# A hybrid decoder block on one core: two more warm-up products, the first weights on the scalar queue, fh and fl at another place in the partition, two orders on TensorE

## The chip, the cores and the metric

The kernel runs on one core of one Trainium2 chip. The metric is the device time of one execution in microseconds; for the kernel before, three runs gave 446.09 to 446.27, median 446.21.

## The reference, cut to what matters

256 tokens, width 1024, float32, one layer:

```
n = rmsnorm(x, norm1_g)
cu, cg, q, k, v, gc, ga = split(n @ w_in)
y_conv = silu(layernorm(causal_conv31(cu * sigmoid(cg)))) @ w_conv_out
y_attn = attention(rmsnorm(q), rmsnorm(k), v, ALiBi, causal, 8 heads of 128) @ w_attn_out
h = x + (sigmoid(gc) * y_conv + sigmoid(ga) * y_attn) @ w_out
out = h + (silu(n2 @ w_gate) * (n2 @ w_up)) @ w_down      # n2 = rmsnorm(h, norm2_g), inner width 2816
```

With 256 tokens in blocks of 256, only a token's own block is attended.

## The kernel before, in words

Every matrix product is made of two token tiles of 128 by chunks of 512 output columns, over k-tiles of 128. For accuracy each operand is split into a high part (rounded to the float32r type) and a low rest, and three products are summed: high by high, low by high, high by low. `mm3` (L133) issues them: the activations (`xh`, `xl`, for example xgh and xgl, or fh and fl) are the stationary operand, the weights (`hi` = whi, `lo` = wlo) move, 512 columns each.

The weights come in pieces of two k-tiles; one piece is one slot of the run loop at the end (L663). In a slot TensorE does six products for token tile 0, then the `jobs` of the slot, then six for token tile 1, then the `post` jobs. `pre` and `late` jobs stand ahead of the slot and behind it. So the place of a job in one of these lists decides where in TensorE's stream its small products break the row of big ones. `stream_dma` (L100) issues the loads of a piece (raw), `stream_split` (L113) makes whi on ScalarE (L123) and wlo on VectorE or POOL (L124), six slots ahead.

The start (L601 to L643) is written out by hand. x comes transposed as xt, in five parts that SP issues between the first weights; the gain of norm1 is an extra column in each of its rows of 257 numbers. `split_x` makes xgh on ScalarE and xgl on VectorE. `square` squares x on ScalarE (sq and xsq, L627 and L630), where xsq of parts 2 and 3 stands behind whi of piece 3, and POOL adds the squares up (L631, L633). `first_norm` is a post job of slot 4: four tiny products ss (L648) sum over the partitions with a column `ones`, which POOL sets at L643. The norm's factor rstd is applied later to the results. Ahead of all this eight warm-up products of zeros (wps, L161) run on TensorE while nothing has landed.

Further places that the change touches: `norm_back` (L299) turns the normalised conv output back with four transposes (yb) for two k-tiles and makes yh and yl of it; four such groups are spread over jobs and post of two slots (L247). `score` (L383) makes the scores sc of a head by two products, a narrow one for query tile 0 and a wide one of 256 columns for query tile 1. In the feed-forward, gu are the gate and up products with hh and hl as stationary operands, dn the down products with fh and fl; the last pieces of dn for token tile 1 are computed in two halves of 256 columns named end.

Where a tile lies in a partition follows from the sizes of the pools, which are laid out one behind the other: constants, weights (raw, whi, wlo), the pairs (xg, y, ao, m, h), small tiles, then the pool of the early stages, whose place is taken by fh and fl later. In the built kernel whi, wlo and the pairs begin at a multiple of 512 bytes, fh and fl 32 bytes behind one.

Of the kernel before, what the change touches and what calls it, by code (L numbers as in the profile page):

```python
# [9 lines left out]
F32 = mybir.dt.float32  # L10
F32R = mybir.dt.float32r
BF16 = mybir.dt.bfloat16
AF = mybir.ActivationFunctionType
# [3 lines left out]
P = 128  # L17
D = 1024
S = 256
T = S // P  # L20
H = 8
KC = 31
FF = 2816
KD = D // P
KF = FF // P
CW = 512
G = 2
EPS = 1e-6
# [13 lines left out]
AHEAD = 6  # L42
# slots after which the next heads follow
HEAD_STEP = ((0, 3, 6, 9), (0, 3, 5, 7))
# weights of the work, by which the taps are dealt out over the slots
SLOT = 2.6
# [4 lines left out]
REFILL = 2  # L51
WARM = 8
TABLE_SLOT = 57


class Chunk:
    """CW output columns of one product, for all tokens: nk k-tiles in pieces of G."""

# [6 lines left out]
def hybrid_block(ctx: ExitStack, tc: tile.TileContext, x, xT, par, w_in, w_co, w_ao, w_o, w_gu, w_dn, out):  # L65
    nc = tc.nc

    cst = ctx.enter_context(tc.tile_pool(name="cst", bufs=1))
    wp = ctx.enter_context(tc.tile_pool(name="wp", bufs=1))
    t8 = ctx.enter_context(tc.tile_pool(name="t8", bufs=2))  # L70
    sm = ctx.enter_context(tc.tile_pool(name="sm", bufs=2))
# [5 lines left out]
    def bank(name, *shape):  # L77
        return ps.tile([P, *shape], F32, tag="tr", bufs=2, name=name)

# [1 line left out]
    slots = []  # L81
# [4 lines left out]
    def add(*chunks):  # L86
        """One chunk, or two of which each half is done in turn."""
        n = chunks[0].nk // G
        parts = [range(n)] if len(chunks) == 1 else [range(n // 2), range(n // 2, n)]
        for part in parts:  # L90
            for c in chunks:
                slots.extend((c, g) for g in part)
# [7 lines left out]
    def stream_dma(upto):  # L100
        while at["dma"] < min(upto, len(slots)):
            i = at["dma"]
            c, g = slots[i]
            raw[i] = wp.tile([P, G, CW], F32, tag="raw", bufs=RAW_BUFS, name=f"raw{i}")
            for part in parts(i):
                nc.sync.dma_start(raw[i][:, part, :], c.w[g][:, part, :])
                between(i, part)
            at["dma"] += 1
# [24 lines left out]
    def mm3(c, i, g, t, acc=None, cols=slice(0, CW), first=0, last=None):  # L133
        """Piece g of the chunk for token tile t; the sum runs from k-tile first to last."""
        xh, xl = c.lhs()
        acc = c.acc[t] if acc is None else acc
        last = c.nk - 1 if last is None else last
        tok = slice(t * P, (t + 1) * P)
        for j in range(G):
            k = g * G + j  # L140
            nc.tensor.matmul(acc, xh[:, k, tok], hi[i][:, j, cols], start=(k == first), stop=False)  # L141
            nc.tensor.matmul(acc, xl[:, k, tok], hi[i][:, j, cols], start=False, stop=False)  # L142
            nc.tensor.matmul(acc, xh[:, k, tok], lo[i][:, j, cols], start=False, stop=(k == last))  # L143

# [1 line left out]
    prm = cst.tile([P, N_PAR], F32, name="prm")  # L146
    xt = ea.tile([P, KD, S + 1], F32, tag="vs", name="xt")
    xs = cst.tile([P, T, D], F32, name="xs")

# [1 line left out]
    warm = cst.tile([P, CW], BF16, name="warm")  # L151
    nc.vector.memset(warm, 0.0)
    tiny = cst.tile([P, 1], F32, name="tiny")

    def load_table(func):
        nc.scalar.activation(tiny, warm[:, :1], func)

    load_table(AF.Sigmoid)
    wps = bank("wps", CW)
    for _ in range(WARM):  # L160
        nc.tensor.matmul(wps, warm[:, :P], warm, start=True, stop=True)  # L161
    ident = cst.tile([P, P], F32, name="ident")
    make_identity(nc, ident)
    mhalf = cst.tile([P, 8], F32, name="mhalf")
    nc.gpsimd.memset(mhalf, -0.5)
# [10 lines left out]
    def rsqrt_mean(o, ss, n, width):  # L176
        """o = (ss / n + EPS) ** -0.5"""
        nc.gpsimd.tensor_scalar(o, ss, 1.0 / n, EPS, op0=ALU.mult, op1=ALU.add)
        nc.gpsimd.tensor_tensor(o, o, mhalf[:, :width], op=ALU.pow)

# [1 line left out]
    xg, aoT, yT, mT, hT = {}, {}, {}, {}, {}  # L182
# [7 lines left out]

# [1 line left out]
    cacc, ca = {}, {}  # L192
# [12 lines left out]
    def refill(ch):  # L205
        """The channels of the next tile go on the partitions, after KC - 1 zeros."""
        j, cv = ch["next"], ch["cv"]
        for t in range(T):
            nc.tensor.transpose(cv[:, KC - 1 + t * P : KC - 1 + (t + 1) * P],
                                ca[j // 2][:, t, (j % 2) * P : (j % 2 + 1) * P], ident)  # L210
        cacc[j] = ea.tile([P, S], F32, tag="cacc", bufs=4, name=f"cacc{j}")
        ch["j"], ch["k"], ch["next"] = j, 0, j + 2
# [11 lines left out]
    def run_taps(slot, until):  # L224
        while load["dve"] + TAP <= until:
            live = [ch for ch in chains if ch["j"] is not None]
            if not live:
                return
            load["turn"] += 1
            ch = live[load["turn"] % len(live)]  # L230
            conv_tap(ch)
            load["dve"] += TAP if len(live) > 1 else TAP_ALONE
            if ch["k"] == KC:
                j, ch["j"] = ch["j"], None
                want_refill(slot, ch)
                if j % 2:
                    last = j == KD - 1
                    at_ = slot + 3
                    while not last and busy[at_] > 1:
                        at_ += 1  # L240
                    busy[at_] += 1
                    jobs[at_].append(lambda p=j // 2: norm_stats(p))
                    pe_side[at_] += 0.45
                    dve_side[at_] += 0.7
                    if last:
                        for i in range(4):
                            (post if i % 2 else jobs)[at_ + 2 + i // 2].append(lambda i=i: norm_back(2 * i))  # L247

# [66 lines left out]

# [1 line left out]
    vs = {}  # L317
# [49 lines left out]
    def head(first, slot, h):  # L367
# [3 lines left out]
        s = {}  # L371
# [11 lines left out]
        def score():  # L383
            s["bias"] = sm.tile([P, 3, P], F32, tag="bias", name=f"bias{h}")
            nc.scalar.mul(s["bias"], dist, 2.0 ** (-8.0 * (h + 1) / H))
            s["sc"] = bank(f"sc{h}", 4, P)
            nc.tensor.matmul(s["sc"][:, 0, :], s["q"][:, :P], s["k"][:, :P], start=True, stop=True)
            nc.tensor.matmul(s["sc"][:, 1:3, :], s["q"][:, P:], s["k"], start=True, stop=True)
            most()
# [50 lines left out]

# [1 line left out]
    sgs = ea.tile([P, 2, T, D], F32, tag="sgs", name="sgs")  # L442
# [21 lines left out]

# [1 line left out]
    def merge_done(b):  # L466
# [26 lines left out]

# [1 line left out]
    s2 = sm.tile([P, T, 2], F32, bufs=1, name="s2")  # L495

# [37 lines left out]

# [1 line left out]
    ff = {}  # L536
# [42 lines left out]

# [1 line left out]
    for p in range(KD // 2):  # L581
# [18 lines left out]

# [1 line left out]
    xg[0] = pair("xg")  # L602

    def load_x(k0, k1):
        nc.sync.dma_start(xt[:, k0:k1, :], xT[:, k0:k1, :])

    def between(i, part):
        if i == 0:
            load_x(part.start, part.stop)
            if part.stop == G:  # L610
                load_x(2, 4)
        elif i < KD // 2 - 1 and part.stop == G:
            load_x(2 * i + 2, 2 * i + 4)

    def split_x(k):
        g = xt[:, k, S:]
        nc.scalar.activation(xg[0][0][:, k, :], xt[:, k, :S], AF.Copy, scale=g)
        nc.vector.scalar_tensor_tensor(xg[0][1][:, k, :], xt[:, k, :S], g, xg[0][0][:, k, :].bitcast(F32),
                                       op0=ALU.mult, op1=ALU.subtract)

    stream_dma(AHEAD)
    sq = ea.tile([P, 2, S], F32, tag="yt", name="sq0")

    def square(q):
        """Squares of x, summed over the parts of its rows that share a partition."""
        if q == 0:
            nc.scalar.activation(sq, xt[:, :2, :S], AF.Square)  # L627
            return
        s = sm.tile([P, 2, S], F32, tag="u", name=f"xsq{q}")
        nc.scalar.activation(s, xt[:, 2 * q : 2 * q + 2, :S], AF.Square)  # L630
        nc.gpsimd.tensor_add(sq, sq, s)  # L631
        if q == KD // 2 - 1:
            nc.gpsimd.tensor_add(sq[:, 0, :], sq[:, 0, :], sq[:, 1, :])  # L633

    for i in range(6):
# [4 lines left out]
        if i >= 2:  # L640
            square(i - 2)
    ones = cst.tile([P, 1], F32, name="ones")
    nc.gpsimd.memset(ones, 1.0)  # L643

    def first_norm():
# [12 lines left out]

# [1 line left out]
    n = len(slots)  # L660
# [85 lines left out]
```

## Time and profile before

| what | |
|---|---|
| time, median of 3 runs | 446.21 us |
| profiled execution, its span from the first to the last instruction | 443.5 us |
| TensorE (PE) busy | 437.6 us, 99% |
| weight loads of TensorE (PEld) busy | 359.6 us |
| VectorE (DVE) busy | 309.6 us |
| ScalarE (ACT) busy | 243.9 us |
| GpSimd (POOL) busy | 87.5 us |
| moved by DMA | 80.21 MB, 181 GB/s on average |

The page gives the span of one profiled execution; the time of a run has in addition what lies around the span, 2.7 us here against the median. Busy times are no proof of a bound by themselves: products are pipelined and overlap in the records, so the distance from one start to the next tells more than a duration. L12 is line 12 of the kernel.

### The profile page before, as it was taken

The page shows a single profiled execution, that of the slowest core. Times are in us where ns is not written, and L with a number is a line of the kernel's source. Part 1 is how long each engine was busy: PE and PEld are TensorE (multiplying, and loading weights), DVE is VectorE, ACT ScalarE, POOL GpSimd, SP SyncE. Part 2 cuts the span into 40 slices and gives each one's busy share as a digit, 9 for nine tenths or more (in the row PEclk, how much of TensorE's full clock was granted, in tenths as well). Part 3 has the DMA queues.
Part 4 walks back from the last instruction along what each step waited for, and adds up shares of the span by engine and source line. Part 5 has one row for each costly group of instructions (what it writes and reads, how often), then busy time and mean ns, then how long its engine had stood idle before and what let it go on. Part 6 is the DMA issues. An engine that isn't in the chain of part 4 may idle for free.

```text
span 443.5 us, 5743 instructions
## 1 busy us (share of the span) xinstructions
PE 437.6 (99%) x2026; PEld 359.6 (81%) x2026; DVE 309.6 (70%) x523; ACT 243.9 (55%) x439; POOL 87.5 (20%) x73
## 2 busy tenths in 40 slices
PE   8999999999999999999999999999999999999997
PEld 4788888888888888888888888888888888888886
DVE  5989999898899799967586575555555555644501
ACT  6854466689998676639325374444444444633200
POOL 1614465745462443100000000000000000000000
PEclk9999999999999999999999999999999999999999
DMA  8986684355345444544837337655555555585001
GB/s 274 345 271 213 211 303 150 144 185 197 142 149 185 142 137 150 190 163 161 293 95 247 133 120 253 196 189 184 184 185 179 187 181 184 184 252 204 25 0 49
DMA packets 23340, 80.21 MB, mean 181 GB/s; under 512 B 2576, under 2 KB 3216, under 8 KB 23312
## 3 DMA queue, kind: packets, MB, share of 16 engines
q1 hardware_dynamic: 22896, 78.66, 52.9%
q10 hardware_dynamic: 416, 1.19, 0.8%
q8 instruction: 16, 0.26, 0.3%
q14 instruction: 12, 0.10, 0.1%
HBM read 78.79 MB, written 1.05 MB: 180 GB/s over the span
## 4 chain that ended last, share of the span: by engine, by line
PE 94%; POOL 2%; ACT 2%; DMA 1%; SPq 0%; issue 0%; DVE 0%
PE gu L141 9%; PE gu L143 9%; PE gu L142 9%; PE dn L141 4%; PE dn L143 4%; PE dn L142 4%; PE g L143 3%; PE g L142 3%; PE g L141 3%; PE conv L141 2%; PE conv L143 2%; PE conv L142 2%; PE k L143 2%; PE v L143 2%; PE q L143 2%; PE q L141 2%
## 5 line engine op out<-in xcount | busy, mean ns | idle before, releaser
L124 DVE TENSOR_TENSOR wlo<-raw,whi 128x1024 fp32r<-128x1024 f32 (+1 forms) x125 | 153.0, 1256 | 30.5 <-ACT whi L123 29.6
L123 ACT CAST whi<-raw 128x1024 fp32r<-128x1024 f32 (+1 forms) x149 | 148.9, 1035 | 34.9 <-PE dn L142 19.8
L221 DVE SCALAR_TENSOR_TENSOR cacc<-cv,prm,cacc 128x256 f32<-128x256 f32 x240 | 97.2, 475 | 0.2
L141 PE MATMUL gu<-whi,hh 128*128 128x512 f32 x176 | 69.6, 395 | 0.0
L124 POOL TENSOR_TENSOR wlo<-raw,whi 128x1024 fp32r<-128x1024 f32 x24 | 58.1, 2426 | 54.5 <-ACT whi L123 49.6
L143 PE MATMUL gu<-wlo,hh 128*128 128x512 f32 x176 | 68.7, 390 | 0.0
L142 PE MATMUL gu<-whi,hl 128*128 128x512 f32 x176 | 68.5, 389 | 0.0
L143 PEld LDWEIGHTS gu<-wlo,hh 128*128 128x128 f32 x176 | 33.0, 188 | 7.1
L142 PEld LDWEIGHTS gu<-whi,hl 128*128 128x128 f32 x176 | 33.1, 188 | 6.6
L141 PEld LDWEIGHTS gu<-whi,hh 128*128 128x128 f32 x176 | 33.1, 188 | 6.4
L141 PE MATMUL dn<-whi,fh 128*128 128x512 f32 x82 | 32.5, 396 | 0.0
L143 PE MATMUL dn<-wlo,fh 128*128 128x512 f32 x82 | 32.4, 396 | 0.0
L142 PE MATMUL dn<-whi,fl 128*128 128x512 f32 x82 | 32.4, 396 | 0.0
L546 ACT ACTIVATE fs<-gu,rstd 128x256 f32<-128x256 f32 x22 | 10.4, 475 | 39.1 <-PE gu L143 39.1
L548 DVE SCALAR_TENSOR_TENSOR f<-gu,rstd,fs 128x256 f32<-128x256 f32 x22 | 10.6, 484 | 29.1 <-ACT fs L546 29.1
L141 PE MATMUL conv<-whi,xgh 128*128 128x512 f32 x64 | 26.1, 409 | 0.9 <-ACT whi L123 0.8
L141 PE MATMUL g<-whi,xgh 128*128 128x512 f32 x64 | 26.6, 415 | 0.0
L142 PE MATMUL conv<-whi,xgl 128*128 128x512 f32 x64 | 25.4, 398 | 0.0
L143 PE MATMUL conv<-wlo,xgh 128*128 128x512 f32 x64 | 25.4, 397 | 0.0
L143 PE MATMUL g<-wlo,xgh 128*128 128x512 f32 x64 | 25.2, 394 | 0.0
L142 PE MATMUL g<-whi,xgl 128*128 128x512 f32 x64 | 25.0, 391 | 0.0
L561 ACT CAST fh<-ftr 128x512 fp32r<-128x512 f32 x11 | 6.5, 587 | 23.9 <-PE ftr L560 23.9
(159 smaller groups left out, 746.4 us busy)
## 6 DMA issues: line engine op xcount, KB each, us to landing
raw<-in_w_in SPq DMA_DIRECT2D x53, 512.0 KB, 4.2
raw<-in_w_gu SPq DMA_DIRECT2D x44, 512.0 KB, 4.3
raw<-in_w_dn SPq DMA_DIRECT2D x22, 512.0 KB, 4.1
raw<-in_w_ao SPq DMA_DIRECT2D x8, 512.0 KB, 3.3
raw<-in_w_co SPq DMA_DIRECT2D x8, 512.0 KB, 3.3
raw<-in_w_o SPq DMA_DIRECT2D x8, 512.0 KB, 5.1
raw<-in_w_in SPq DMA_DIRECT2D x6, 256.0 KB, 4.7
xs<-in_x ACTq DMA_DIRECT2D x1, 1024.0 KB, 4.7
```

The lines of the kernel that those rows point to most:

```text
L123: nc.scalar.copy(hi[i][:, part, :], r[:, part, :])
L124: eng.tensor_sub(lo[i][:, part, :], r[:, part, :], hi[i][:, part, :].bitcast(F32))
L141: nc.tensor.matmul(acc, xh[:, k, tok], hi[i][:, j, cols], start=(k == first), stop=False)
L142: nc.tensor.matmul(acc, xl[:, k, tok], hi[i][:, j, cols], start=False, stop=False)
L143: nc.tensor.matmul(acc, xh[:, k, tok], lo[i][:, j, cols], start=False, stop=(k == last))
L221: nc.vector.scalar_tensor_tensor(cacc[j], src, w, cacc[j], op0=ALU.mult, op1=ALU.add)
L546: nc.scalar.activation(sg, acc[t][:, :256], AF.Silu, scale=r)
L548: nc.vector.scalar_tensor_tensor(f[t], acc[t][:, 256:], r, sg, op0=ALU.mult, op1=ALU.mult)
L561: nc.scalar.copy(fh[:, k2, :], tr)
```

## The change

It sets ten warm-up products instead of eight and makes their tile smaller (128 columns, read four times). The first half of the first weights is issued on ScalarE's queue, ahead of the load of the function table; SP starts with x. x is laid out with the eight gains in 16 columns in front and rows of 256 numbers behind. `ones` is set among POOL's first constants. The four groups of norm_back all become jobs, two to a slot. The wide score product comes before the narrow one. A tile s2 of 16 bytes is made 512 bytes long. Through the sizes of warm, the constants and s2, whi, wlo, the pairs and fh and fl all begin 256 bytes behind a multiple of 512 in the built kernel.

```diff
-WARM = 8
+WARM = 10
+XG = 16
 ...
             for part in parts(i):
-                nc.sync.dma_start(raw[i][:, part, :], c.w[g][:, part, :])
+                if i == 0:
+                    load_x(part.start, part.stop)
+                (nc.sync if i or part.start else nc.scalar).dma_start(raw[i][:, part, :], c.w[g][:, part, :])
                 between(i, part)
 ...
-    xt = ea.tile([P, KD, S + 1], F32, tag="vs", name="xt")
+    xt = ea.tile([P, XG + KD * S], F32, tag="vs", name="xt")
 ...
-    warm = cst.tile([P, CW], BF16, name="warm")
+    warm = cst.tile([P, P], BF16, name="warm")
 ...
-    load_table(AF.Sigmoid)
-    wps = bank("wps", CW)
+    wps = bank("wps", 4, P)
     for _ in range(WARM):
-        nc.tensor.matmul(wps, warm[:, :P], warm, start=True, stop=True)
+        nc.tensor.matmul(wps, warm, warm[:, None, :].to_broadcast([P, 4, P]), start=True, stop=True)
     ident = cst.tile([P, P], F32, name="ident")
     make_identity(nc, ident)
+    ones = cst.tile([P, 1], F32, name="ones")
+    nc.gpsimd.memset(ones, 1.0)
 ...
                         for i in range(4):
-                            (post if i % 2 else jobs)[at_ + 2 + i // 2].append(lambda i=i: norm_back(2 * i))
+                            jobs[at_ + 2 + i // 2].append(lambda i=i: norm_back(2 * i))
 ...
+            nc.tensor.matmul(s["sc"][:, 1:3, :], s["q"][:, P:], s["k"], start=True, stop=True)
             nc.tensor.matmul(s["sc"][:, 0, :], s["q"][:, :P], s["k"][:, :P], start=True, stop=True)
-            nc.tensor.matmul(s["sc"][:, 1:3, :], s["q"][:, P:], s["k"], start=True, stop=True)
 ...
-    s2 = sm.tile([P, T, 2], F32, bufs=1, name="s2")
+    s2 = sm.tile([P, 128], F32, bufs=1, name="s2")[:, : 2 * T].rearrange("p (t b) -> p t b", b=2)
 ...
+    def xk(k0, k1):
+        return xt[:, XG + k0 * S : XG + k1 * S].rearrange("p (k s) -> p k s", s=S)
+
     def load_x(k0, k1):
-        nc.sync.dma_start(xt[:, k0:k1, :], xT[:, k0:k1, :])
+        cols = slice(XG + k0 * S if k0 else 0, XG + k1 * S)
+        nc.sync.dma_start(xt[:, cols], xT[:, cols])
 ...
     stream_dma(AHEAD)
+    load_table(AF.Sigmoid)
 ...
-    ones = cst.tile([P, 1], F32, name="ones")
-    nc.gpsimd.memset(ones, 1.0)
```

How the built order moves, at the places the prediction speaks of. First SP's queue at the start; raw is a piece of weights, xt a part of x. Before:

```order
L106 DMA raw_121<-in_w_in 128x512
L605 DMA xt<-in_xT 128x257
L106 DMA raw_121<-in_w_in 128x512
L605 DMA xt<-in_xT 128x257
L605 DMA xt<-in_xT 128x514
L106 DMA raw_127<-in_w_in 128x512 x2
```

After:

```order
L613 DMA xt<-in_xT 128x272
L613 DMA xt<-in_xT 128x256
L109 DMA raw_124<-in_w_in 128x512
L613 DMA xt<-in_xT 128x512
L109 DMA raw_130<-in_w_in 128x512 x2
```

The first half piece has left SP's queue, both first parts of x stand ahead of the second half, and everything behind moves up by one transfer. On ScalarE's queue it stands first. Before:

```order
L156 ACT_TABLE_LOAD
L156 ACTIVATE tiny<-warm 128x1
L617 ACTIVATE xgh<-xt 128x256
L123 CAST whi_142<-raw_121 128x512
```

After:

```order
L109 DMA raw_124<-in_w_in 128x512
L159 ACT_TABLE_LOAD
L159 ACTIVATE tiny<-warm 128x1
L624 ACTIVATE xgh<-xt 128x256
L126 CAST whi_146<-raw_124 128x512
```

So the table load comes behind one issue. Last, TensorE where the normalised conv output is turned back, in the products ao of the attention's output projection (ao_0 and ao_1 are the two token tiles). Before:

```order
L307 MATMUL yb_2135<-ident,yt 128x128 x4
L141 MATMUL ao_1_2100<-whi_2017,aoh 128x512
...
L143 MATMUL ao_1_2100<-wlo_2018,aoh 128x512
L307 MATMUL yb_2151<-ident,yt 128x128 x4
L141 MATMUL ao_0_2099<-whi_2038,aoh 128x512
```

After:

```order
L311 MATMUL yb_2137<-ident,yt 128x128 x4
L311 MATMUL yb_2147<-ident,yt 128x128 x4
L144 MATMUL ao_1_2102<-whi_2019,aoh 128x512
...
L146 MATMUL ao_0_2101<-wlo_2040,aoh 128x512
L311 MATMUL yb_2175<-ident,yt 128x128 x4
L311 MATMUL yb_2185<-ident,yt 128x128 x4
```

Four groups with six big products between each became two pairs with twelve between them.

## Rows read from the trace of the kernel before

**Rows 1.** The page's part 4: the chain that ended last, by engine

```profile
PE 94%; POOL 2%; ACT 2%; DMA 1%; SPq 0%; issue 0%; DVE 0%
```

**Rows 2.** Waits of TensorE: line, releaser, us in total, times, longest

```profile
PE wps L161 <- DVE warm L152: 1.2, 1, 1.2
PE conv L141 <- ACT whi L123: 0.8, 1, 0.8
PE ss L648 <- POOL ones L643: 0.5, 1, 0.5
```

**Rows 3.** The chain in order of time, 0 to 23: start us, us, what

```profile
2.10 4.17 DMA xt<-in_xT
...
12.42 0.94 ACT whi L123
...
13.97 1.81 POOL sq L631
...
20.32 1.60 POOL sq L633
```

**Rows 4.** Timeline of TensorE around ss: start us, us, what

```profile
21.09 0.39 PE L143 MATMUL conv<-wlo,xgh 128*128 128x512 f32 x1
22.01 0.61 PE L648 MATMUL ss<-ones,sq 128*128 128x1 f32 x4 [0.53 <-POOL ones L643]
```

**Rows 5.** Timeline of TensorE, the first 10 us

```profile
1.18 3.60 PE L161 MATMUL wps<-warm 128*128 128x512 bf16 x8 [1.18 <-DVE warm L152]
...
7.95 0.63 PE L142 MATMUL conv<-whi,xgl 128*128 128x512 f32 x1
...
9.23 0.44 PE L142 MATMUL conv<-whi,xgl 128*128 128x512 f32 x1
...
9.96 0.40 PE L142 MATMUL conv<-whi,xgl 128*128 128x512 f32 x1
```

**Rows 6.** Stretches: busy of PE, PEld, DVE, ACT, POOL; PEclk, DMA share, GB/s

```profile
2.00:4.00 2.00, 2.00 (x6) 0.76 (x5) 0.00 (x0) 0.20 (x1) 0.45 (x2) 1.00 0.93 270
4.00:6.00 2.00, 1.18 (x3) 0.41 (x2) 0.91 (x2) 1.02 (x2) 0.00 (x0) 1.00 0.87 240
6.00:8.00 2.00, 1.88 (x5) 0.89 (x4) 1.41 (x4) 1.71 (x4) 0.00 (x0) 1.00 1.02 364
```

**Rows 7.** Timeline of TensorE, gate/up stage, two products 24 apart

```profile
262.76 0.39 PE L143 MATMUL gu<-wlo,hh 128*128 128x512 f32 x1
...
268.20 0.39 PE L143 MATMUL gu<-wlo,hh 128*128 128x512 f32 x1
```

**Rows 8.** Timeline of TensorE, down stage, two products 24 apart

```profile
390.07 0.40 PE L143 MATMUL dn<-wlo,fh 128*128 128x512 f32 x1
...
395.67 0.40 PE L143 MATMUL dn<-wlo,fh 128*128 128x512 f32 x1
```

**Rows 9.** The page's part 5: one of the three groups of the down stage

```profile
L141 PE MATMUL dn<-whi,fh 128*128 128x512 f32 x82 | 32.5, 396 | 0.0
```

**Rows 10.** Timeline of SP's queue at the start

```profile
0.72 0.38 SPq L106 DMA_DIRECT2D raw<-in_w_in  x1
1.16 0.42 SPq L605 DMA_DIRECT2D xt<-in_xT  x1
```

**Rows 11.** Timeline of TensorE and ScalarE around the first two yb groups

```profile
197.43 0.39 PE L143 MATMUL ao<-wlo,aoh 128*128 128x512 f32 x1
...
198.32 0.40 PE L142 MATMUL ao<-whi,aol 128*128 128x512 f32 x1
...
199.49 0.60 PE L307 MATMUL yb<-ident,yt 128*128 128x128 f32 x4
...
200.12 1.02 ACT L311 ACTIVATE sl<-yb,prm 128x256 f32<-128x256 f32 x2
```

**Rows 12.** Timeline around one score

```profile
143.71 0.38 PE L387 MATMUL sc<-kT,qT 128*128 128x128 f32 x2
...
144.60 0.40 PE L142 MATMUL g<-whi,xgl 128*128 128x512 f32 x1
```

More of the change, by code (lines that the diff above doesn't have):

```diff
@@ L602, in hybrid_block @@
     xg[0] = pair("xg")
+    def xk(k0, k1):
+        return xt[:, XG + k0 * S : XG + k1 * S].rearrange("p (k s) -> p k s", s=S)
     def load_x(k0, k1):
-        nc.sync.dma_start(xt[:, k0:k1, :], xT[:, k0:k1, :])
+        cols = slice(XG + k0 * S if k0 else 0, XG + k1 * S)
+        nc.sync.dma_start(xt[:, cols], xT[:, cols])
     def between(i, part):
         if i == 0:
-            load_x(part.start, part.stop)
             if part.stop == G:
@@ L615, in split_x @@
     def split_x(k):
-        g = xt[:, k, S:]
-        nc.scalar.activation(xg[0][0][:, k, :], xt[:, k, :S], AF.Copy, scale=g)
-        nc.vector.scalar_tensor_tensor(xg[0][1][:, k, :], xt[:, k, :S], g, xg[0][0][:, k, :].bitcast(F32),
+        g, one = xt[:, k : k + 1], slice(k, k + 1)
+        nc.scalar.activation(xg[0][0][:, one, :], xk(k, k + 1), AF.Copy, scale=g)
+        nc.vector.scalar_tensor_tensor(xg[0][1][:, one, :], xk(k, k + 1), g, xg[0][0][:, one, :].bitcast(F32),
                                        op0=ALU.mult, op1=ALU.subtract)
     stream_dma(AHEAD)
+    load_table(AF.Sigmoid)
     sq = ea.tile([P, 2, S], F32, tag="yt", name="sq0")
@@ L626, in square @@
         if q == 0:
-            nc.scalar.activation(sq, xt[:, :2, :S], AF.Square)
+            nc.scalar.activation(sq, xk(0, 2), AF.Square)
             return
         s = sm.tile([P, 2, S], F32, tag="u", name=f"xsq{q}")
-        nc.scalar.activation(s, xt[:, 2 * q : 2 * q + 2, :S], AF.Square)
+        nc.scalar.activation(s, xk(2 * q, 2 * q + 2), AF.Square)
         nc.gpsimd.tensor_add(sq, sq, s)
@@ L725 @@
         "x": x,
-        "xT": np.concatenate([x.T, i["norm1_g"].reshape(D, 1)], axis=1).reshape(KD, P, S + 1).transpose(1, 0, 2),
+        "xT": np.concatenate([vec(i["norm1_g"]), np.zeros((P, XG - KD), np.float32),
+                              x.T.reshape(KD, P, S).transpose(1, 0, 2).reshape(P, KD * S)], axis=1),
         "par": par,
```

## The prediction

> **What bounds the kernel now.** Start with the page's shares of the chain that ended last [rows 1]: 94% of it is TensorE's own work. So the question is not which engine, but where TensorE waits and how fast its products follow each other. Its waits [rows 2] are three, all early: 1.2 us for the zeros of the warm-up products, 0.8 us for the first weights, 0.5 us in front of ss (the sums for the first norm). After 22.5 us it waits for nobody. From there only the distance between two products counts.
>
> Next read the chain in order of time [rows 3]. Up to 22 us it does not run on TensorE: the second part of x lands at 6.27, then ScalarE works without a hole (copies of x and weights, sq, whi of piece 3, xsq) until POOL begins at 13.97; POOL adds the squares in four steps to 21.92, and ss can start at 22.01. TensorE's own rows there [rows 4]: the last conv product before ss starts at 21.09, ss at 22.01. With the usual 0.23 to the next start it could have gone at 21.32, so 0.69 us is lost. This is the point to keep: **whatever makes TensorE earlier before 21.3 us is swallowed at ss, unless POOL's sum comes earlier too.**
>
> The first rows of TensorE [rows 5] show why one would want more warm-up products. The eight take 3.60 us, then comes the hole of 0.8. Of the conv products three go from 7.95 to 9.23, 0.43 us each; the next three take 0.73 in all, 0.24 each. 512 columns in 0.43 us is the lower clock level, 1.2 GHz; behind 9.5 us it is the upper one. (The granted clock in the stretches [rows 6] reads 1.00 throughout and does not resolve this.)
>
> Last, the distance of two products in the steady stages. In the gate/up stage 24 products go from 262.76 to 268.20, 0.2267 us each [rows 7]; in the down stage 24 go from 390.07 to 395.67, 0.2333 us each [rows 8]. Shapes are the same. In the built kernel before, whi, wlo and the pairs xg, ao, y, m, h begin at a multiple of 512 bytes in the partition; fh and fl begin 32 bytes past one. After the change all of them begin 256 bytes past one, fh and fl too, so the distance between stationary and moving tile is a multiple of 512 everywhere.
>
> **The change, part by part.**
>
> *fh and fl.* 3 x 82 = 246 products of 512 columns read them [rows 9]. If they take the distance of the gate/up stage, 246 x 0.0066 = **-1.6 us**, all of it on the path, since TensorE waits for nothing there. From nothing to this are the bounds. I take the full value: the slow distance sets in with the first product on fh and holds in every product on either tile. The 36 products of 256 columns at the end read them too: half of 0.0066 on 36 is **-0.1** (bounds 0 and -0.2).
>
> The Trainium skill, page TensorE: Matmul & The Clock Gate, section Step-by-step: what each phase is for, speaks against this term: TensorE has two independent read ports into SBUF, and loading the next weights doesn't take bandwidth from the running product. By it the distance would not depend on where the tiles lie, and this term would be 0. The trace differs, 0.2267 against 0.2333, and I go by the trace.
>
> *Start: warm-up products, queue of the first weights, x.* Two more warm-up products at 0.43 run to about 5.4 us, inside the old hole. Today the first product waits 0.8 us for whi behind eight of them, so two more, 0.85 us, delay it by nothing that is still seen at ss. They may bring the upper level earlier: the eight products before 9.23 could each save up to 0.2. I cost all this at 0: it is covered by the wait at ss. If that cover were gone it would be worth up to 1.6.
>
> What counts is when POOL can begin, and that is whi of piece 3 on ScalarE, 12.42 in the chain. SP issues its second transfer 0.44 us behind its first [rows 10], and so on. With piece 0's first half on ScalarE's queue every transfer behind it is issued one step earlier; x parts 0 and 1 gain one and two. On ScalarE the issue (0.38 as on SP) pushes the table load behind it by as much; ScalarE's next work waits for x, today until after 4 us, so this is covered. Were x there at 2 us, it would cost the 0.38. But the DMA engines are already 0.93 busy from 2 us and full from 6 us [rows 6]: an earlier issue helps only as far as they had nothing to do, or moved badly. Bounds: 0, if they were simply full; 1.6, if one step of 0.44 is gained and the stretch from 2 to 6 us (540 and 480 KB, some 1.02 MB in 4 us) goes at the 364 GB/s of 6 to 8 us, 2.8 us. That second half is possible because x's rows are no longer 1028 bytes but 1024 or 1088, which no longer start at odd places. I take one step, **-0.4 us**, the row nearest to it. The ones for ss were set on POOL behind the sum, which ends at 21.92, and ss waits for them until 22.01 [rows 2 to 4]; moved to the front they are **-0.1** on the same path. So ss starts near 21.5, and TensorE, at 21.3 even if it gained nothing, is there first. The next thing late is still POOL. VectorE's rstd and the first conv gate follow the same chain and shift with it.
>
> *The four yb groups* (transposes of the normalised conv output). Today four breaks, one in front of each half slot; afterwards two with eight transposes. One break [rows 11]: the ao product before starts at 197.43, the second one behind at 198.32. Two products are 0.45 of these 0.89 us, which leaves 0.44 for four transposes, 0.11 each, their 128 columns at the products' own pace. The five products that follow take 1.17 instead of 5 x 0.2267 = 1.13. So a break costs about 0.04 besides its work, and two fewer give **-0.1** (bounds 0 and -0.1). The second group of a pair needs its bank read. For k2 = 2 that is the bank of ytr, whose reads lie before the first group. For k2 = 6 ScalarE reads k2 = 2 today from 200.12 on, for 1.02 us, and would do so a little sooner; it is asked for behind the group that starts at about 201.3, so it is free. Were it not, ScalarE's next such pair of 1.02 us is the most that TensorE would wait.
>
> *Scores.* One case [rows 12]: from the first of the narrow pair, 143.71, to the second product behind the wide pair, 144.60, it is 0.89 us. At the 0.11 per 128 columns of the transposes, two passes of 128 and two of 256 columns are 0.66, and one product is 0.23. Nothing is left over that an order could save, so turned round it is the same: 0. I allow 0.02 for each of 8 heads, 0.15 either way, about half of what a yb break costs. All small tiles change place too; for some 180 transposes I allow 0.25 either way.
>
> **Sum:** -1.6 - 0.1 - 0.4 - 0.1 - 0.1 = -2.3 us. The span becomes 441.2; 446.21 (median of three runs) lies 2.7 above the profiled span, and that stays: **443.9 us**. Its own range, with start 0 to -1.0 and the small terms at their ends, is 443.2 to 444.7.
>
> **Rivals.**
> *B, fh and fl bring nothing.* The down stage then keeps 0.2333 for another cause (it has its own load of VectorE and ScalarE, and other weights). Only start and yb remain: 445.6. This is what the page's rule on two ports would make of the term. Against it: the change of distance sets in exactly with the tile. 0.12.
> *C, the start gives all its bound,* because x's odd rows held the transfers up: -1.6 instead of -0.4 in that term, 442.7 with the small terms. POOL would end near 20.3, and TensorE has to be there first, so the upper clock level would have to come earlier too. 0.10.
> *D, slower: the place itself decides, not the distance.* All fast products of the trace have both operands at 0 modulo 512; 256 was never seen there. If any place but 0 costs 0.0066, the 1488 products of the other stages (14 chunks of the input product, 6 of ao, co and wo, 11 of gate/up, 48 products each) lose 9.8 us and the down stage wins nothing: 455.4. It decides as soon as more than 350 of the 1488 products slow down. Against it: two readers that get in each other's way are a matter of distance. 0.05.
> *E, a longer wait in front of ss lets the clock fall.* TensorE, earlier by up to 1.6, could wait 1.8 us there instead of 0.69, and start again at the lower level. If that lasted as long as the eight warm-up products, 3.6 us at 0.43 a product, it would be 8 products of 0.2 more, 1.7 us: 445.6. Against it: the wait of today is followed by distances of 0.23. 0.05.
>
> **How the numbers follow.** The forecast has 0.68. About 0.2%, 0.9 us, is what a measurement of this kernel can tell from no change: below 445.3 is faster, above 447.1 slower. Forecast and C make faster 0.78; B and E lie within, 0.17; D is slower, 0.05. The range takes in the forecast, B and E, with C and D left out (0.15): 443.0 to 445.7.
>
> **What would show it.** Right: products in the down stage 0.2267 apart; the other stages unchanged; ss near 21.5, still behind POOL, with a longer wait of TensorE in front; two yb breaks; score places of the same length. Wrong: 0.2333 left in the down stage (B), 0.2333 anywhere else (D), ss before 21 (C), 0.43 apart behind ss (E). If ss starts at 22.0 again, the start term was 0.

## The result, and the profile after

The changed kernel takes 443.59 us (median of 4 runs, 443.47 to 443.91), the kernel before 446.15 us beside it (445.76 to 446.27): ratio 0.9946, 95% interval 0.9932 to 0.996, 2.56 us less. The forecast was 443.9, with a range of 443.0 to 445.7.

First the down stage. The timeline of TensorE, two products 24 apart as in [rows 8]:

```profile
390.20 0.39 PE L144 MATMUL dn<-whi,fh 128*128 128x512 f32 x1
...
395.64 0.39 PE L144 MATMUL dn<-whi,fh 128*128 128x512 f32 x1
```

5.44 us for 24, 0.2267 each, where it was 0.2333. The gate/up stage, two products 24 apart as in [rows 7], now with its operands at 256 and not at 0:

```profile
262.99 0.39 PE L146 MATMUL gu<-wlo,hh 128*128 128x512 f32 x1
...
268.43 0.39 PE L146 MATMUL gu<-wlo,hh 128*128 128x512 f32 x1
```

Again 5.44: no other stage pays for the new place.

Now the start. TensorE's waits (line, releaser, us in total, times, longest), as [rows 2]:

```profile
PE ss L653 <- POOL sq L641: 1.9, 1, 1.9
PE wps L163 <- DVE warm L155: 1.0, 1, 1.0
PE conv L144 <- ACT whi L126: 0.5, 2, 0.3
```

Its timeline, the first 10 us and around ss, as [rows 4, 5]:

```profile
0.97 3.98 PE L163 MATMUL wps<-warm 128*128 128x512 bf16 x10 [0.97 <-DVE warm L155]
5.15 0.51 PE L144 MATMUL conv<-whi,xgh 128*128 128x512 f32 x1 [0.19 <-ACT whi L126]
...
8.02 0.40 PE L145 MATMUL conv<-whi,xgl 128*128 128x512 f32 x1
8.25 0.39 PE L146 MATMUL conv<-wlo,xgh 128*128 128x512 f32 x1
...
20.24 0.39 PE L146 MATMUL conv<-wlo,xgh 128*128 128x512 f32 x1
22.54 0.60 PE L653 MATMUL ss<-ones,sq 128*128 128x1 f32 x4 [1.91 <-POOL sq L641]
```

The conv products run at the upper level now: those at 8.02 and 8.25 are 0.23 apart, where 0.43 stood. (That the two additional warm-up products did it isn't shown: with eight and the same start, warm8 below has them 0.23 apart by 7.12 us.) TensorE is 0.85 us earlier in front of ss (20.24, not 21.09), and waits there 1.4 us longer. The chain in order of time, as [rows 3], says for whom:

```profile
2.10 5.60 DMA xt<-in_xT
7.72 0.91 ACT xgh L624 x2
...
13.00 0.94 ACT whi L126
...
14.55 1.81 POOL sq L639
...
20.89 1.60 POOL sq L641
```

In this execution the third transfer of x lands at 7.70 and ScalarE starts on it at 7.72. Everything behind follows without a hole, whi of piece 3 at 13.00 instead of 12.42, POOL at 14.55 instead of 13.97. So ss comes 0.53 us later than in the profile of before, not earlier. SP's queue shows that a late issue was not the cause (as [rows 10]):

```profile
0.72 0.86 SPq L613 DMA_DIRECT2D xt<-in_xT  x2
1.63 0.42 SPq L109 DMA_DIRECT2D raw<-in_w_in  x1
2.10 0.43 SPq L613 DMA_DIRECT2D xt<-in_xT  x1
```

That part of x left SP's queue at 2.10, one step earlier than before, and landed later: before, ScalarE began on it at 7.21 and found it there. The first two parts were issued earlier as well and did land earlier: ScalarE began on them at 4.08 and 5.00 us, before at 4.53 and 6.29.

Last the yb transposes, as [rows 11]:

```profile
197.74 0.39 PE L146 MATMUL ao<-wlo,aoh 128*128 128x512 f32 x1
197.97 1.03 PE L311 MATMUL yb<-ident,yt 128*128 128x128 f32 x8
...
199.07 0.40 PE L145 MATMUL ao<-whi,aol 128*128 128x512 f32 x1
```

Eight transposes and two products in 1.33 us: 0.45 for the products leave 0.11 per transpose, as before, in half as many breaks.

By stages, in us, each from its first product to the first one of the next (in the row "start", from 0 to ss; q is the second q chunk, end runs to the end of the span):

| | start | ss to q | q to ao | ao to co | co to gu | gu to dn | dn | end | span |
|---|---|---|---|---|---|---|---|---|---|
| before | 22.01 | 64.55 | 95.66 | 24.11 | 46.23 | 125.39 | 57.84 | 7.68 | 443.48 |
| after | 22.54 | 64.55 | 95.45 | 24.03 | 46.23 | 125.38 | 56.23 | 7.74 | 442.13 |

The two profiles differ by 1.35 us, the medians by 2.56. In every run of the changed kernel and of the experiments the time is 1.8 us above its span. So the profiled execution of before was one of about 445.3, at the fast end of that kernel (445.4 to 446.3 in most executions), and the profiled one of after is the slowest of its four, 443.91. Each kernel has one profile, so what differs between its executions isn't seen directly; between the profiles it is where ss starts and, in some, TensorE's clock behind it, while stages with their tiles at the same places repeat to a few hundredths.

### The profile page after: what moved, and what is told of

It is laid out like the page before. It is cut to its first block, busy times and chain, and to the rows that moved or that the text cites. A ratio compares the mean times of both kernels' runs of the same rounds, so it can differ in the third digit from the quotient of the medians.

```text
span 442.1 us, 5748 instructions
## 1 busy us (share of the span) xinstructions
PE 435.4 (98%) x2028; PEld 359.0 (81%) x2028; DVE 309.3 (70%) x523; ACT 243.9 (55%) x439; POOL 87.4 (20%) x73
## 4 chain that ended last, share of the span: by engine, by line
PE 94%; POOL 2%; ACT 2%; DMA 1%; SPq 0%; issue 0%; DVE 0%
PE gu L144 9%; PE gu L146 9%; PE gu L145 9%; PE dn L146 4%; PE dn L144 4%; PE dn L145 4%; PE g L146 3%; PE g L144 3%; PE g L145 3%; PE conv L144 2%; PE conv L146 2%; PE conv L145 2%; PE k L146 2%; PE k L144 2%; PE v L146 2%; PE q L146 2%
```

## The experiments

The kernels ran in three groups, each on a chip of its own beside runs of the kernel before: place_alone, place_undone, place_256 and wide_alone; weights_on_sp, x_rows_257, warm8 and ss_later; narrow_first, warm_0, place_64 and all_32. Medians are compared within a group, and by their ratio to the kernel before across groups.

**place_alone**: the kernel before, only s2 longer. Weights and pairs stay at 0 modulo 512, fh and fl go from 32 to 0.

```diff
-    s2 = sm.tile([P, T, 2], F32, bufs=1, name="s2")
+    s2 = sm.tile([P, 128], F32, bufs=1, name="s2")[:, : 2 * T].rearrange("p (t b) -> p t b", b=2)
```

> The kernel before with s2 made 512 bytes long and nothing else: fh and fl move from 32 bytes past a multiple of 512 to a multiple, the weights stay at a multiple. My theory (the distance between stationary and moving tile decides): products of the down stage 0.2267 us apart instead of 0.2333, time 444.5 (446.15 - 1.6). Rival B (two read ports, the place cannot matter): 0.2333, 446.1.

444.12 us against 445.9 of before (ratio 0.9971, 0.9949 to 0.9993). Down stage 56.23, stretch from q to ao 95.44, end 7.73: -1.61, -0.22 and +0.05 are -1.78, all of the difference of the medians. One line, which makes a tile of 16 bytes longer, brings most of the change.

**place_undone**: the changed kernel with the short s2; weights at 256, fh and fl at 288.

```diff
-    s2 = sm.tile([P, 128], F32, bufs=1, name="s2")[:, : 2 * T].rearrange("p (t b) -> p t b", b=2)
+    s2 = sm.tile([P, T, 2], F32, bufs=1, name="s2")
```

> The changed kernel with the short s2: fh and fl lie again 32 bytes further on than the weights modulo 512 (288 against 256), all else as changed. My theory: 0.2333 us between products of the down stage, time 445.2 (443.6 + 1.6). If the change's gain came from something else (rival B): 0.2267 or an unchanged 443.6.

446.86 us, ratio 1.0011 (0.9999 to 1.0024). The down stage is back at 57.84. But 1.6 is not the whole loss: behind ss the stretch to q takes 66.14 instead of 64.55. The 12 runs fall into two groups, three at 445.0 to 445.5 and nine at 446.7 to 447.3, and the profile is of the second.

**place_256**: s2 of 256 bytes, so that weights lie at 256 and fh and fl at 0.

```diff
-    s2 = sm.tile([P, 128], F32, bufs=1, name="s2")[:, : 2 * T].rearrange("p (t b) -> p t b", b=2)
+    s2 = sm.tile([P, 64], F32, bufs=1, name="s2")[:, : 2 * T].rearrange("p (t b) -> p t b", b=2)
```

> The changed kernel with s2 of 256 bytes: fh and fl at a multiple of 512, the weights 256 bytes past one, so the distance is 256 modulo 512. If any distance but 0 modulo 512 costs: 0.2333 us or more in the down stage, 445.2 or more. If only parts of 64 or 256 bytes matter: 0.2267, 443.6. I expect the first, at 0.6.

445.08 us, ratio 0.9967 (0.9953 to 0.9981); down stage 56.23. So a distance of 256 costs nothing, and "modulo 512" was too strict. Here too there are two groups (five runs at 443.4 to 443.8, seven at 445.1 to 445.5), and the profile, of the second group (ss to q 66.16), shows why. Timeline of TensorE behind ss:

```profile
22.09 0.61 PE L653 MATMUL ss<-ones,sq 128*128 128x1 f32 x4 [2.00 <-POOL sq L641]
22.55 0.63 PE L144 MATMUL conv<-whi,xgh 128*128 128x512 f32 x1
22.98 0.63 PE L145 MATMUL conv<-whi,xgl 128*128 128x512 f32 x1
23.41 0.63 PE L146 MATMUL conv<-wlo,xgh 128*128 128x512 f32 x1
```

And the granted clock (PEclk, third column from the end) in stretches of 2 us:

```profile
20.00:22.00 2.00, 0.08 (x1) 0.00 (x0) 2.00 (x2) 0.32 (x1) 1.92 (x2) 1.00 0.83 240
22.00:24.00 2.00, 1.91 (x8) 1.63 (x9) 2.00 (x2) 0.72 (x1) 0.03 (x1) 0.68 0.82 252
24.00:26.00 2.00, 2.00 (x7) 1.51 (x6) 1.45 (x3) 0.00 (x0) 0.47 (x1) 0.50 0.79 246
26.00:28.00 2.00, 2.00 (x10) 1.65 (x9) 0.99 (x4) 1.72 (x4) 0.71 (x3) 0.97 1.00 293
```

After 2.00 us of waiting the products are 0.43 apart, 1.2 GHz, for 8 products of 0.2 more: 1.6 us. That is rival E, at about the price named for it (1.7). It doesn't follow each such wait: after waits 1.91 in its profile and goes on at 0.23.

**wide_alone**: the kernel before with the wide score product first.

```diff
-            nc.tensor.matmul(s["sc"][:, 0, :], s["q"][:, :P], s["k"][:, :P], start=True, stop=True)
             nc.tensor.matmul(s["sc"][:, 1:3, :], s["q"][:, P:], s["k"], start=True, stop=True)
+            nc.tensor.matmul(s["sc"][:, 0, :], s["q"][:, :P], s["k"][:, :P], start=True, stop=True)
```

> The kernel before with the wide score product first and nothing else. The prediction put this at 0, within 0.15 either way; the trace of the changed kernel shows the stretch from the second q chunk to ao 0.21 us shorter and the products behind a score 0.31 and then 0.227 apart, where they were 0.42 and then 0.23 to 0.236. If the order does it: that stretch 0.2 us shorter, time 445.9. If the shift of small tiles did it: 446.15 and the old distances.

445.55 us against 445.9, ratio 0.999 (0.9975 to 1.0004): not told from no change. From q to ao 95.56, 0.10 less than before.

**narrow_first**: the changed kernel with that order turned back.

> The changed kernel with the narrow score product first again. Theory PLACE (the attention stretch became shorter by 0.21 us because its small tiles lie elsewhere): from the second q chunk to ao 95.45 as in the changed kernel, time 443.6. Rival ORDER (the wide product first saves 0.1 of it): 95.55, 443.7.

443.78 us against 445.84, ratio 0.9968 (0.9951 to 0.9984); from q to ao 95.49. By the profiles the order is worth 0.04 here, 0.10 there; the rest of the 0.21 goes with the place, as place_alone showed. (Four of the ten runs lie apart, at 445.05 to 446.4.)

**weights_on_sp**: the changed kernel with the first half piece on SP's queue again, ahead of x.

```diff
+                nc.sync.dma_start(raw[i][:, part, :], c.w[g][:, part, :])
                 if i == 0:
                     load_x(part.start, part.stop)
-                (nc.sync if i or part.start else nc.scalar).dma_start(raw[i][:, part, :], c.w[g][:, part, :])
```

> The changed kernel with the first half piece of weights issued on SP again, in the order of before (weights, x, weights, x); all else as changed. In the changed kernel's profile ss came at 22.54, later than before (22.01), not earlier as predicted. If the second queue is what slowed the landings: ss near 22.0, time 443.1. If it saves an issue step as predicted: ss 0.4 later than in the changed kernel, 444.0. If the landings at the start merely differ from run to run: no difference beyond 0.3.

444.02 us against 445.99, ratio 0.9957 (0.9941 to 0.9974). ss at 22.63. The chain runs over another part of x:

```profile
3.98 5.70 DMA xt<-in_xT
9.71 0.91 ACT xgh L624 x2
```

The time is the one expected if the second queue saves an issue step, but ss is only 0.09 later than in after, on another chip, and 0.68 later than in warm8 below, on this one. One profile of each doesn't decide it.

**x_rows_257**: the changed kernel with x in rows of 257 numbers and its gain as their last column, as before.

```diff
-    xt = ea.tile([P, XG + KD * S], F32, tag="vs", name="xt")
+    xt = ea.tile([P, KD, S + 1], F32, tag="vs", name="xt")
...
-        cols = slice(XG + k0 * S if k0 else 0, XG + k1 * S)
-        nc.sync.dma_start(xt[:, cols], xT[:, cols])
+        nc.sync.dma_start(xt[:, k0:k1, :], xT[:, k0:k1, :])
```

> The changed kernel with x laid out as before (rows of 257 numbers with the gain at the end), all else as changed. If the odd rows slow the transfers (rival C): raw of piece 3 lands later, ss 0.3 to 1 us later, time 444 to 444.6. If the layout does nothing: 443.6.

444.64 us, ratio 0.9967 (0.9954 to 0.998); first conv product at 6.29 instead of 5.15, ss at 22.94. Two pieces of the chain in order of time:

```profile
0.72 4.88 DMA raw<-in_w_in
...
6.47 5.47 DMA xt<-in_xT
```

In warm8, on the same chip, that first half piece takes 3.33 us, and ScalarE begins on x at 3.76, here at 5.1. So ss, and nearly the time, are those expected if the odd rows slow the transfers.

**warm8**: the changed kernel with eight warm-up products (`WARM = 8`).

> The changed kernel with eight warm-up products. The prediction says what the warm-up products bring is swallowed at ss: ss where it is in the changed kernel, TensorE's wait there 1.9 us or less, time 443.6. If they count: up to 1.6 us slower, 445.2.

443.35 us (443.28 to 443.41), ratio 0.9937 (0.9924 to 0.995): no slower than ten; ss at 21.95. The upper level comes as early as with ten:

```profile
0.97 3.60 PE L163 MATMUL wps<-warm 128*128 128x512 bf16 x8 [0.97 <-DVE warm L155]
...
7.12 0.39 PE L145 MATMUL conv<-whi,xgl 128*128 128x512 f32 x1
7.35 0.40 PE L146 MATMUL conv<-wlo,xgh 128*128 128x512 f32 x1
```

Six of six runs lie below every run of weights_on_sp (443.62 to 445.56) and of x_rows_257 (443.56 to 446.69) on the same chip. So the queue seems worth some tenths, the rows as much or more, though two warm-up products fewer are a difference as well.

**warm_0**: no warm-up products at all (`WARM = 0`).

> The changed kernel without any warm-up product. Theory SWALLOWED (whatever TensorE gains before ss it waits for there): its first conv products run 0.43 apart for longer, the last one before ss starts between 20.3 and 21.5 instead of 20.24, ss still waits for POOL near 22.5, time 443.2 to 443.8. Rival NEEDED (warm-up products are worth what they bring): the lower level lasts 3.6 us longer, 8 products of 0.2 more each, TensorE comes to ss after POOL, time 444.5 to 445.2.

443.46 us (443.33 to 443.71), ratio 0.9946 (0.9929 to 0.9963): the ratio of the changed kernel with its ten. Timeline of TensorE:

```profile
10.30 0.63 PE L145 MATMUL conv<-whi,xgl 128*128 128x512 f32 x1
10.72 0.53 PE L146 MATMUL conv<-wlo,xgh 128*128 128x512 f32 x1
11.09 0.39 PE L144 MATMUL conv<-whi,xgh 128*128 128x512 f32 x1
...
21.77 0.39 PE L146 MATMUL conv<-wlo,xgh 128*128 128x512 f32 x1
22.32 0.61 PE L653 MATMUL ss<-ones,sq 128*128 128x1 f32 x4 [0.16 <-POOL sq L641]
22.79 0.48 PE L144 MATMUL conv<-whi,xgh 128*128 128x512 f32 x1
23.10 0.39 PE L145 MATMUL conv<-whi,xgl 128*128 128x512 f32 x1
```

The lower level lasts until 11 us, TensorE arrives 1.5 us later than in after, and is still in time: ss waits 0.16 for POOL. What TensorE gains before ss is swallowed there. None of these four runs has the 1.6 us more, as one would expect of a short wait; but four are few, and warm8 with its wait of 2.0 has none in six.

**ss_later**: the changed kernel with ss, and with it the first conv gate, one slot of 12 products later.

```diff
-            first = slot + (2 if p == 0 else 1)
+            first = slot + (3 if p == 0 else 1)
...
-    post[4].append(first_norm)
+    post[5].append(first_norm)
```

> The changed kernel with the first norm's sums ss one slot later (post of slot 5) and the first conv gate one slot later. TensorE then reaches ss 2.7 us later, behind POOL's sum. If the wait at ss swallows what the start won: the 1.9 us wait goes, time 441.7 to 442. If something else holds TensorE after 22 us (psum banks, the gate, the taps): the wait comes back there, 443.6.

442.81 us against 445.99, ratio 0.9936 (0.9915 to 0.9956); span 440.8. It is the lowest median here, on the chip on which warm8 took 443.35, though the intervals overlap. TensorE around ss:

```profile
22.50 0.39 PE L146 MATMUL conv<-wlo,xgh 128*128 128x512 f32 x1
22.73 0.50 PE L653 MATMUL ss<-ones,sq 128*128 128x1 f32 x4
```

The wait is gone, with ss 0.23 behind the product ahead of it; only now does the early start count. But not all of it arrives, and 442.81 is above the 441.7 to 442 expected. The products ao start 2.54 us earlier than in after (180.00, not 182.54), the products gu only 1.37 (251.42, not 252.79): from ao to gu it takes 71.42 us instead of 70.25. The second pair of yb groups now stands among the products co, and the first products there wait for yl, as this row of TensorE's waits shows:

```profile
PE co L145 <- DVE yl L318: 0.2, 1, 0.2
```

The rows beside it hold the rest: the products co from 203.23 to 204.29 are 0.73 and 0.33 apart, and those from 210.00 to 210.82 are 0.49 and 0.33 apart, instead of 0.23. So the second alternative of the expectation holds in part: 1.2 us of the wait came back later.

**place_64** and **all_32** tell what about the place decides: the distance between stationary and moving tile, or where fh and fl themselves begin. place_64 is the changed kernel with s2 of 64 bytes (weights at 256, fh and fl at 320). all_32 is the kernel before with the long s2 and one constant more, so that weights, pairs, fh and fl all lie at 32.

```diff
-    s2 = sm.tile([P, 128], F32, bufs=1, name="s2")[:, : 2 * T].rearrange("p (t b) -> p t b", b=2)
+    s2 = sm.tile([P, 16], F32, bufs=1, name="s2")[:, : 2 * T].rearrange("p (t b) -> p t b", b=2)
```

```diff
+    pad = cst.tile([P, 8], F32, name="pad")
+    nc.gpsimd.memset(pad, 0.0)
...
-    s2 = sm.tile([P, T, 2], F32, bufs=1, name="s2")
+    s2 = sm.tile([P, 128], F32, bufs=1, name="s2")[:, : 2 * T].rearrange("p (t b) -> p t b", b=2)
```

> The changed kernel with s2 of 64 bytes instead of 512: weights and pairs stay 256 behind a multiple of 512, fh and fl go to 320, 64 bytes behind them. Theory DISTANCE (a product is slowed where stationary and moving tile are an odd small distance apart; 0 and 256 were fast, 32 slow): dn products more than 0.2267 apart, between that and 0.2333, the down stage longer than 56.23 us, up to 57.84. Rival ALIGNMENT (what counts is that fh and fl themselves begin at a multiple of 64 bytes, whatever the weights do; 320 is one, the 32 and 288 of the slow kernels are not): 0.2267 as in the changed kernel, 56.23.

> The kernel before with one constant of 32 bytes more and s2 of 512 bytes, so that weights, pairs and fh and fl all begin 32 behind a multiple of 512: the distance is 0, the place of everything is what fh and fl alone had before. Theory DISTANCE: 0.2267 in every stage, about 444.1 as with s2 alone. Rival ALIGNMENT: 0.2333 in every stage, 1488 x 0.0066 = 9.8 us more outside the down stage and nothing gained in it, gate/up stage 125.4 to 129, time near 456.

place_64: 446.87 us, ratio 1.0019 (1.0002 to 1.0036). Timeline, 24 products apart:

```profile
390.06 0.39 PE L146 MATMUL dn<-wlo,fh 128*128 128x512 f32 x1
...
395.66 0.39 PE L146 MATMUL dn<-wlo,fh 128*128 128x512 f32 x1
```

5.60, 0.2333 each; down stage 57.84, as with a distance of 32. (Its clock fell behind ss too: from there to q 66.16.) all_32: 444.56 us, ratio 0.9968 (0.9957 to 0.9978):

```profile
390.05 0.39 PE L143 MATMUL dn<-wlo,fh 128*128 128x512 f32 x1
...
395.49 0.39 PE L143 MATMUL dn<-wlo,fh 128*128 128x512 f32 x1
```

5.44, and gate/up takes 125.42: with everything at 32, nothing is slow. The distance decides. 0 and 256 are free, 32 and 64 cost the same 0.0066 per product; 128 was not tried. Of the 512-column products only those on fh and fl had their distance varied.

## Why the prediction was right, point by point

**fh and fl: right, in size and reason.** -1.6 predicted, -1.61 measured in after, place_alone and place_256, and gone again in place_undone and place_64. Too strict was only that the distance has to be a multiple of 512: 256 does as well. Rival B falls with it, and rival D too: at a common 256 or a common 32 all stages run at 0.2267. The Trainium skill, page TensorE: Matmul & The Clock Gate, section Step-by-step: what each phase is for, says that loading the next weights takes nothing from the running product, since the ports are two. The runs differ: same shapes, same instructions, 0.2267 or 0.2333 by the distance alone. Why the distance costs time, and whether it is the weight load that takes it, no run shows.

**End products: wrong sign.** -0.1 predicted. Their stage is 7.68 before, 7.74 after, and 7.52 at a distance of 64. The tile's instructions (nanoseconds min/median/max) in before, in after and in place_64:

```profile
L141 PE MATMUL end<-whi,fh x12: 277/280/285, 435.8 to 439.7; 128*128 128x256 f32 x12
```

```profile
L144 PE MATMUL end<-whi,fh x12: 278/283/284, 434.4 to 438.3; 128*128 128x256 f32 x12
```

```profile
L144 PE MATMUL end<-whi,fh x12: 276/276/281, 437.2 to 440.9; 128*128 128x256 f32 x12
```

So for 256 columns the distances rank differently, and 0 and 256 are the slowest (7.73 and 7.74 in place_alone and place_256). The step that failed is "half of 0.0066 on 36": a rate of one shape was carried to another.

**Start: the swallowing was right, the size is only inferred.** Predicted were 0 for the warm-up products, and warm_0 and warm8 show just that. For the queue, x and the ones it was -0.5, with ss near 21.5. No profile shows ss there (nor before 21, as rival C had it), and that of after shows 22.54. Over the profiles, ss starts at 22.01 to 23.17 with the old start (before, place_alone, wide_alone, all_32; mean 22.5), at 21.85 to 22.54 with the new one (after, place_undone, place_256, place_64, narrow_first, warm8, warm_0; mean 22.2): the right direction, with a scatter larger than the difference. By the medians, -2.56 less the -1.78 of place_alone and the -0.08 of yb leaves about -0.7, part of which is the score order; the two medians come from different chips. The step "one step of 0.44, the row nearest to it" took an earlier issue for an earlier landing. Each part of x was issued a step or more earlier, the first two landed earlier for it, but the third, from which the chain of after runs, landed at 7.70 and so later than before. Which part is late differs between the profiles: in weights_on_sp and x_rows_257 the chain runs from the fourth and the fifth. That the size of the whole start came out near the forecast is therefore in part luck. Of the rows, rival C's cause, x_rows_257 says that they matter: with the old ones ss is 0.4 us later than in after and 1.0 later than in warm8. The ones brought half of their 0.1: ss starts 0.05 behind POOL's sum in after, 0.09 in before.

**Scores and small tiles: 0 predicted, -0.21 measured,** inside the allowance of 0.25. place_alone and all_32 have it with the old order (95.44), place_64 lacks it with the new one (95.67): it goes with the place that s2 sets. Which of the small products gain stays open.

**yb: right.** -0.1 predicted, -0.08 measured.

**What lies around the span: wrong, without effect.** Not 2.7 but 1.8; the rest was that the profile of before is of one of its fastest executions. As the forecast is the median less a difference, this cancels.

**Rival E: priced right, its chance too small.** 0.05 was given because the wait of before does no harm. The four runs of after escape it, but of the 42 runs with the same start in place_undone, place_256, place_64 and narrow_first 26 lie in the group of the longer times, and the three profiles taken from it show the clock fall behind the wait. The mean granted clock of the runs agrees: it is 0.991 to 0.996 in all of the 26, and 0.999 or 1.0 in 14 of the 16 others. In these three profiles the wait is 1.95 to 2.0 us; it was 0.5 in before and 1.5 in place_alone, and both go on at 0.23. What decides isn't settled: warm8 waits 2.0 as well, and its six runs are undisturbed. Nor is the kernel before quite free of it: 8 of its 73 runs beside the experiments take over 447 us, with a mean clock of 0.996, and none of them was profiled.

## What to carry to other kernels

Where two stages have the same products and one is slower by a steady few per cent, look at where their operands lie in the partition: padding one small tile moved 246 products by 0.0066 us each. Work that makes an engine earlier in front of a wait brings nothing until the wait's other side is earlier too, or the waiting instruction stands later (ss_later); it can even cost, where TensorE's clock falls in the longer wait. An instruction that is moved back moves what hangs on it, and part of the wait can come back there (1.2 us in ss_later). And one profile of each kernel is not enough to attribute half a microsecond, if a transfer at the start lands up to a microsecond apart between profiles with the same start (ScalarE begins on the third part of x at 7.72 in after, at 6.72 in place_64).

## What the runs showed of the hardware that was not expected

- The 512-column products of the down stage follow each other at 0.2267 us where stationary and moving tile are 0 or 256 bytes apart modulo 512, and at 0.2333 where it is 32 or 64; the common base (0, 32, 256) doesn't matter. With 256 columns the order is another: their stage is shortest at 64 (7.52), longest at 0 and 256 (7.74).
- Behind a wait of 2.0 us TensorE ran, in some executions, at 1.2 GHz for 8 products (1.6 us more), with PEclk 0.68 and 0.50 in the stretches 22 to 24 and 24 to 26 us of place_256. In all_32 the clock fell early, behind two waits for whi of 0.75 and 0.87 us, and what it cost was swallowed before ss (first the stretch, then PEclk as the third column from the end):

```profile
8.00:10.00 2.00, 2.00 (x6) 1.37 (x5) 2.00 (x5) 1.41 (x3) 0.00 (x0) 0.57 1.04 359
10.00:12.00 2.00, 2.00 (x6) 1.57 (x6) 1.61 (x4) 1.89 (x4) 0.00 (x0) 0.57 1.06 422
```

- With the same start and ten warm-up products the granted clock rises at 4.4 us in after, inside the warm-up products, and at 5.7 in place_256, behind them. The Trainium skill, page TensorE: Matmul & The Clock Gate, section Part 1: The HAM clock gate (the "warmup" mystery), says that the same kernel changes level after a different number of products from run to run; the traces agree, as far as two kernels with one start can show it.
